# Counting tensor instructions per fetched block in a build-time scheduler, and placing dense matmuls where the next block would be late

## The chip, the cores and the metric

The kernel runs on all eight cores of one Trainium2 chip, one sequence per core; nothing passes between the cores. The metric is the device time in microseconds (us) of the slowest core. Every execution is also recorded core by core: the span from first to last instruction and the granted clock of TensorE.

Executions have two states. In the slow one, the cores of one die (cores 0 to 3 or 4 to 7) show a lower granted clock than the others and the time is longer: the kernel before took 3630.3 us in a fast execution, 3772.86 in one where the four cores of die 0 had a clock of 0.94, and 4275.75 where they had 0.81. Where single cores are compared, they come from *undisturbed dies*, those in which all four cores had a granted clock of 0.981 or more.

Engine names: PE is TensorE's matmul, PEld its weight load, DVE is VectorE, ACT is ScalarE, POOL is GpSimd, SP is SyncE.

## The reference, cut to what matters

Four layers of a hybrid decoder trunk, D = 1024, feed-forward width 2816, 8 prompts of 2048 tokens and 128 single-token samples.

```python
def _layer(x, ...):
    h = _rmsnorm(x, norm1_g)
    z = h @ w_in                          # dense, 1024 -> 4096
    zb, zc, zv, zu, ga, gs = split(z)
    conv_out, new_buf = _conv_causal(zc * zv, conv_buf, conv_w, conv_b)
    ya = zb * conv_out
    ys, hr, hi = _s5(zu, ...)             # diagonal state space: 32 groups, 64 complex states each
    gy = gelu(ys)
    ys = gy * sigmoid(gy @ w_glu + b_glu)
    m = sigmoid(ga) * (ya @ w_branch[:512]) + sigmoid(gs) * (ys @ w_branch[512:])
    x = x + m @ w_out                     # dense
    h2 = _rmsnorm(x, norm2_g)
    gate, up = split(h2 @ w_gate_up)      # dense, 1024 -> 5632
    return x + (silu(gate) * up) @ w_down # dense
    ...
```

Nearly all arithmetic is in the dense products. The state space (SSM) part is little arithmetic in many small matmuls.

## The kernel before

A core works through its 2048 columns in two halves of 1024; the first half also carries 16 sample columns. The kernel's Python code does not emit instructions directly. It records *operations*, each with an estimated duration, its dependences and its buffers. An operation of TensorE is a group of matmuls. `schedule()` then simulates the five engines and fixes every engine's instruction order at build time.

The scheduler picks the ready operation of the best priority that has room for its results:

```python
    def schedule(self):
        ...
        def feasible(o, t):
            ...
                if fr not in tls:     # out of the program's order: keep `reserve` buffers free
                    if p.reserve < 0 or len(free) - len(tls) < p.reserve:
                        return False
            ...
        while nleft:
            ...
                while a and n < 60:
                    item = heapq.heappop(a)
                    o = item[2]
                    n += 1
                    if feasible(o, t):
                        ...
                        pick = o
                        break
                    put.append(item)
            ...
            o = pick
            dur = o.dur
            ...
            o.start = t
            efree[e] = t + dur
            ...

    PP = Pool("psum", 8, lambda s: PSUM[s], reserve=3)
```

There are two kinds of TensorE operation. A dense one has typically 8 matmuls of 128x272, 128x384 or 128x512:

```python
    def proj(parts, blk, own=()):
        ps = PP.new()
        nmm = len(parts)
        subs = []
        for i, (u, kw, c, src, keys) in enumerate(parts):
            subs.append((lambda e, ...: e.matmul(
                ps[:, 0:blk.n], lhsT=u.ap(kw, c), rhs=src(blk), start=(i == 0), stop=(i == nmm - 1)),
                [u.key] + keys(blk) + list(own), MMN(blk.n)))
        S.pe(subs, [(ps,)], FULL)
```

An SSM quarter (four a layer and half) has up to six operations of many tiny matmuls, 152 in all in the first half:

```python
            # L1043: 32 matmuls of 64 columns       L1053: 16 of 16 columns (samples)
            S.pe(subs, [(gg,)], (128, 64))
            ...                                   # DVE: rotate, scan, rotate back
            # L1090/L1093: 16 of 128 and 64 columns L1103/L1107: 24 of 16 columns (samples)
            S.pe(subs, [(yb[0],), (yb[1],)], FULL)
            ...
            # L1117: 64 of 64 columns
            S.pe(subs, [(yb[0],), (yb[1],)], (64, 128))
```

Each matmul is two instructions, a weight load and a multiply (23,772 records of each on core 1 of the kernel before). So 256 instructions are 128 matmuls. By the medians of that core's trace they are 27 us of dense 128x512 ones (216 ns from one to the next), but only 2 to 7 us of the small ones (15 to 56 ns from one to the next).

Of the kernel before, what the change touches and what calls it, by code (L numbers as in the profile page):

```python
# [76 lines left out]
class Prog:  # L77
# [3 lines left out]
    SWITCH = 1.28  # L81
    MODESW = 0.16
    DBW = 300.0e3
    NSEM = {"sp": 14, "pool": 8}

    def __init__(self):
# [91 lines left out]
    def schedule(self):  # L178
        ops = self.ops
        for o in ops:  # L180
            o.succ = []
            o.ready = 0.0
        for o in ops:
            o.npred = len(o.deps)
            for d, i in o.deps:
                d.succ.append((o, i))
        for p in {id(tl.pool): tl.pool for o in ops for tl in o.tiles}.values():
            p.tiles.sort(key=lambda tl: tl.users[0].seq)
        self.order = {e: [] for e in self.ENGS}
        fut = {e: [] for e in self.ENGS}  # L190
        avail = {e: [] for e in self.ENGS}
        efree = {e: 0.0 for e in self.ENGS}
        curset = None
        curmode = None
        lastpe = None
        bus = 0.0
        dcount = {"sp": 0, "pool": 0}
        dlast = {}
        events = []
        ctr = 0  # L200

        def push(t, e):
            nonlocal ctr
            ctr += 1
            heapq.heappush(events, (t, ctr, e))
        for o in ops:
            if o.npred == 0:
                heapq.heappush(fut[o.eng], (0.0, o.seq, o))
        for e in self.ENGS:
            push(0.0, e)  # L210
        nleft = len(ops)
        pos = {e: 0 for e in self.ENGS}
        inorder = {e: [o for o in ops if o.eng == e] for e in self.ENGS}

        def feasible(o, t):
            need = {}
            for tl in o.tiles:
                if tl.slot is None:
                    need.setdefault(tl.pool, []).append(tl)
            for p, tls in need.items():  # L220
                free = p.free
                if len(free) < len(tls):
                    return False
                fr = p.tiles[p.front] if p.front < len(p.tiles) else None
                if fr not in tls:
                    if p.reserve < 0 or len(free) - len(tls) < p.reserve:
                        return False
                elif p.reserve < 0:
                    for k_ in range(len(tls)):
                        if p.tiles[p.front + k_] not in tls:  # L230
                            return False
            return True
        while nleft:
            if not events:
                rem = [o for o in ops if not o.done]
                raise RuntimeError("stuck: %s" % [(o.seq, o.eng, o.npred, [(t.pool.name, t.idx, t.slot) for t in o.tiles]) for o in rem[:12]])
            t, _, e = heapq.heappop(events)
            if isinstance(e, tuple):
                p, s = e
                p.free.append(s)  # L240
                for e2 in self.ENGS:
                    if efree[e2] <= t:
                        push(t, e2)
                continue
            if efree[e] > t + 1e-9:
                continue
            f, a = fut[e], avail[e]
            while f and f[0][0] <= t + 1e-9:
                _, _, o = heapq.heappop(f)
                heapq.heappush(a, (o.prio, o.seq, o))  # L250
            pick = None
            if LISTSCHED:
                put = []
                n = 0
                best_sw = None
                while a and n < 60:
                    item = heapq.heappop(a)
                    o = item[2]
                    n += 1
                    if feasible(o, t):  # L260
                        sw = (e == "act" and o.tset is not None and o.tset != curset)
                        if sw and best_sw is None and n < 6:
                            best_sw = item
                            put.append(item)
                            continue
                        if sw and best_sw is not None:
                            put.append(item)
                            continue
                        if best_sw is not None and o.prio > best_sw[0] + SWW:
                            put.append(item)  # L270
                            break
                        pick = o
                        break
                    put.append(item)
                if pick is None and best_sw is not None:
                    pick = best_sw[2]
                    put.remove(best_sw)
                for item in put:
                    heapq.heappush(a, item)
            else:  # L280
                if pos[e] < len(inorder[e]):
                    o = inorder[e][pos[e]]
                    if a and any(x[2] is o for x in a) and feasible(o, t):
                        a[:] = [x for x in a if x[2] is not o]
                        heapq.heapify(a)
                        pick = o
                        pos[e] += 1
            if pick is None:
                if f:
                    push(f[0][0], e)  # L290
                continue
            o = pick
            dur = o.dur
            if e == "act" and o.tset is not None and o.tset != curset:
                dur += self.SWITCH
                curset = o.tset
            if e == "pe":
                if curmode is not None and o.mode != curmode:
                    dur += self.MODESW
                    o.forced = lastpe  # L300
                curmode = o.mode
                lastpe = o
            o.start = t
            efree[e] = t + dur
            if o.dma:
                q = dcount[e]
                dcount[e] = q + 1
                o.sem = (e, q % self.NSEM[e])
                o.semprev = dlast.get(o.sem)
                dlast[o.sem] = o  # L310
                beg = max(bus, t + dur + 0.6)
                bus = beg + o.nbytes / self.DBW
                o.end = bus + 1.3 + o.extra
            else:
                o.end = t + dur
            o.done = True
            nleft -= 1
            self.order[e].append(o)
            for tl in o.tiles:
                if tl.slot is None:  # L320
                    p = tl.pool
                    tl.slot = p.free.pop(0)
                    tl.prev = p.last[tl.slot]
                    while p.front < len(p.tiles) and p.tiles[p.front].slot is not None:
                        p.front += 1
                tl.left -= 1
                tl.end = max(tl.end, o.end)
                if tl.left == 0:
                    p = tl.pool
                    p.last[tl.slot] = tuple(tl.users)  # L330
                    push(tl.end + self.LAT, (p, tl.slot))
            for s, i in o.succ:
                s.npred -= 1
                r = o.end + (0.0 if e == "pe" and s.eng == "pe" else self.LATPE if s.eng == "pe" else self.LAT) - s.offs[i]
                if r > s.ready:
                    s.ready = r
                if s.npred == 0:
                    heapq.heappush(fut[s.eng], (s.ready, s.seq, s))
                    push(max(s.ready, t, efree[s.eng]), s.eng)
            push(efree[e], e)  # L340
        self.makespan = max(o.end for o in ops)
# [120 lines left out]
def build():  # L462
# [69 lines left out]
    sems = {e: es.enter_context(nc.semaphore(f"s_{e}")) for e in Prog.ENGS}  # L532
    dsems = {(e, i): es.enter_context(nc.semaphore(f"d_{e}{i}")) for e in Prog.NSEM for i in range(Prog.NSEM[e])}

# [892 lines left out]
```

## Time and profile before

| | before |
|---|---|
| time, median of 3 runs | 3630.3 us (3630.3 to 3638.21) |
| span of the slowest core (core 1) and of the fastest | 3626.0 and 3611.5 us |
| PE busy, core 1 | 3473.9 us, 96% |
| PE waits called "issue", core 1 | 22.9 us, 0.6% |
| PE instruction records, core 1 | 51,257 = 200.2 x 256 |

Lines of the profile page of the kernel before, core 1: the span, the busy time of each engine (share of the span, number of instructions), the queue that brings instructions (packets, MB, share of 16 DMA engines), and the chain of waits that ended last.

```profile
span 3626.0 us, 67081 instructions; the slowest of 8 cores (3611.5 to 3626.0 us)
...
PE 3473.9 (96%) x23772; PEld 1960.4 (54%) x23772; DVE 1691.4 (47%) x3029; ACT 1147.2 (32%) x2158; POOL 609.1 (17%) x799
...
q8 instruction: 200, 3.28, 0.4%
...
PE 87%; DVE 4%; issue 4%; DMA 2%; ACT 2%; SPq 1%; DVEq 0%; POOL 0%; ACTq 0%; POOLq 0%
```

The kernel is bound by TensorE, and about 150 us of the span are not PE. The list of PE's waits on core 1 says what ended them; the columns are the total, how often, and the longest.

```profile
PE ps L712 <- ACT H L710: 22.7, 10, 8.9
PE ps L905 <- DVE SC L562: 14.9, 7, 4.3
...
PE ps L670 <- DMA R<-dy: 14.2, 5, 8.9
PE ps L670 <- issue: 7.6, 4, 3.0
...
PE ps L1117 <- issue: 3.5, 1, 3.5
PE ps L1103 <- issue: 3.5, 1, 3.5
PE ps L1053 <- issue: 3.1, 1, 3.1
```

"issue" means that PE waited for nothing that the profile shows. These waits are few and long. The timeline of PE on core 1 shows two of them; the columns are start, duration, line, operation and its tiles, and in brackets the idle time before it.

```profile
586.66 0.19 PE L1107 MATMUL ps<-AS0Z,TAB 128*128 128x16 bf16 x2
590.34 0.18 PE L1103 MATMUL ps<-UU,TAB 128*128 128x16 bf16 x1 [3.48 <-issue]
...
590.74 3.95 PE L670 MATMUL ps<-H,RING 128*128 128x272 bf16 x16
...
595.93 0.82 PE L1117 MATMUL ps<-VT,TAB 64*128 64x64 bf16 x44
600.28 0.47 PE L1117 MATMUL ps<-VT,TAB 64*128 64x64 bf16 x20 [3.53 <-issue]
```

The pauses fall in the *middle* of operations (after 44 of 64 matmuls of one kind), and the profile shows nothing that the next matmul waits for. Counting PE's records from 0, the first instructions after the two pauses are records 9403 (the weight load of the matmul shown) and 9659: exactly 256 apart. All eight pauses of over 1.5 us on core 1 are at records that leave 187 when divided by 256. The queue that brings instructions moved 200 packets of 16,384 bytes each, 3.28 MB in all, for 51,257 records, which is 200.2 blocks of 256. So the trace shows instructions coming in blocks of 256, a packet each. They come while PE works: a packet starts about when the block before its own begins (2.6 us after, see fetchpace). PE paused for over 1.5 us at eight of the 200 block ends on core 1, and each of the eight blocks before these ends is made mostly of small matmuls: 88 to 126 of them, and 2.6 to 7.4 us of work by my estimate, the usual distances of its matmuls in this trace summed (the blocks before the pauses at 600 and 1520 us hold 4.1 and 2.8 us). The block before 600 us in fact took 6.4 us on core 1: after the pause that ends at 590.34, PE's granted clock is 0.60 in 590.7 to 594.8 us, and the 16 matmuls of 128x272 take 3.95 us, against 2.39 us for 16 such at 1512.5 us, where the clock is 1.00.

### The profile page before, as it was taken

To read this page: it belongs to the slowest core of one execution; us is meant where nothing else is said; L and a number is where in the kernel's file an instruction comes from. 1 tells how busy PE (TensorE), PEld (TensorE's weight loads), DVE (VectorE), ACT (ScalarE), POOL (GpSimd) and SP (SyncE) were. 2 spreads that over 40 slices of the span, in tenths; PEclk is the share of its full clock that TensorE was granted. 3 is DMA by queue.
4 is the path that set the end of the run, shared out by engine and by line. 5 is a ranking of instruction groups with operands and counts; after the bars stand their busy time and mean duration, and the time that the engine had idled before them with its cause. 6 is when DMAs were issued, how large, how long until landed. Compare 5 with 4: busy or idle time off the path is not lost.

```text
span 3626.0 us, 67081 instructions; the slowest of 8 cores (3611.5 to 3626.0 us)
## 1 busy us (share of the span) xinstructions
PE 3473.9 (96%) x23772; PEld 1960.4 (54%) x23772; DVE 1691.4 (47%) x3029; ACT 1147.2 (32%) x2158; POOL 609.1 (17%) x799
## 2 busy tenths in 40 slices
PE   6899998999999999999999899999999999999998
PEld 3566666666666666666664344444444444444443
DVE  8856455465554754644245342454214542254423
ACT  4543134432343322533134330233203431142302
POOL 4233210322103221020000200002000110002000
PEclk9899999999999999999999999999999999999999
DMA  8645677445574355854439544574445734464443
GB/s 160 127 71 75 113 156 139 82 71 114 138 148 84 69 115 126 184 123 86 74 60 209 114 82 70 96 171 76 77 75 115 155 67 80 76 138 85 81 70 88
DMA packets 252805, 384.13 MB, mean 106 GB/s; under 512 B 157632, under 2 KB 180800, under 8 KB 246848
## 3 DMA queue, kind: packets, MB, share of 16 engines
q0 software_dynamic: 67968, 243.30, 40.8%
q1 hardware_dynamic: 184512, 136.53, 12.9%
q8 instruction: 200, 3.28, 0.4%
q14 instruction: 125, 1.02, 0.1%
HBM read 567.06 MB, written 56.12 MB: 172 GB/s over the span
## 4 chain that ended last, share of the span: by engine, by line
PE 87%; DVE 4%; issue 4%; DMA 2%; ACT 2%; SPq 1%; DVEq 0%; POOL 0%; ACTq 0%; POOLq 0%
PE ps L670 83%; DMA dy<-YY 1%; PE ps L1117 1%; DVE H L736 1%; ACT SC L1233 1%; PE ps L707 1%; DVE SC L562 1%; PE ps L1043 1%; PE ps L1090 1%; PE ps L918 0%; DMA scv<-CIN 0%; DVE R L1235 0%; SPq L633 0%; PE ps L905 0%; DMA R<-dy 0%
## 5 line engine op out<-in xcount | busy, mean ns | idle before, releaser
L670 PE MATMUL ps<-H,RING 128*128 128x384 bf16 (+2 forms) x12160 | 2196.5, 340 | 30.1 <-DVE H L736 14.2
L670 PEld LDWEIGHTS ps<-H,RING 128*128 128x128 bf16 x12160 | 1191.3, 99 | 973.2 <-issue 57.4
L670 PE MATMUL ps<-R,RING 128*128 128x384 bf16 (+2 forms) x6400 | 1162.4, 338 | 24.2 <-DMA R<-dy 14.2
L670 PEld LDWEIGHTS ps<-R,RING 128*128 128x128 bf16 x6400 | 623.5, 98 | 525.5 <-issue 44.6
L657 POOL DMA_DIRECT2D RING<-wpk x472 | 253.1, 537 | 2588.2 <-PE ps L670 2330.0
L1278 DVE TENSOR_TENSOR R<-SC,ps 128x384 bf16<-128x384 f32 (+2 forms) x440 | 255.1, 583 | 755.0 <-PE ps L670 722.3
L1277 ACT ACTIVATE SC<-ps 128x384 f32<-128x384 f32 (+2 forms) x440 | 225.8, 515 | 1167.9 <-PE ps L670 1152.1
L1256 DVE TENSOR_TENSOR X<-X,ps 128x384 f32<-128x384 f32 (+2 forms) x480 | 271.0, 581 | 386.8 <-PE ps L670 384.8
L705 ACT ACTIVATE SC<-X 128x384 f32<-128x384 f32 (+2 forms) x280 | 147.2, 543 | 205.0 <-DVE X L1256 178.7
L736 DVE SCALAR_TENSOR_TENSOR H<-X,PRM,SC 128x384 bf16<-128x384 f32 (+2 forms) x304 | 190.9, 698 | 27.4 <-ACT SC L717 27.4
L1250 POOL TENSOR_TENSOR R<-TB,SC 128x384 bf16<-128x384 f32 (+1 forms) x160 | 167.8, 1064 | 101.0 <-DVE SC L1247 85.9
L1247 DVE TENSOR_TENSOR SC<-SC,ps 128x384 f32<-128x384 f32 (+1 forms) x160 | 92.7, 584 | 141.4 <-PE ps L670 68.1
L1246 ACT ACTIVATE SC<-ps 128x384 f32<-128x384 f32 (+1 forms) x160 | 81.4, 515 | 235.0 <-PE ps L670 194.9
L1223 DVE TENSOR_TENSOR TB<-TB,ps 128x384 f32<-128x384 f32 (+2 forms) x160 | 90.0, 583 | 128.9 <-PE ps L670 111.3
L562 DVE TENSOR_TENSOR SC<-TB 128x512 f32<-128x512 f32 (+1 forms) x160 | 121.1, 767 | 5.6
L1182 DVE TENSOR_TENSOR CIN<-ps,SC 128x384 f32<-128x384 f32 (+2 forms) x80 | 46.9, 586 | 156.1 <-ACT SC L1181 146.4
L1168 ACT ACTIVATE TB<-ps 128x384 f32<-128x384 f32 (+1 forms) x160 | 79.6, 516 | 100.1 <-PE ps L670 99.7
L562 POOL TENSOR_TENSOR TB<-TB 128x512 f32<-128x512 f32 (+1 forms) x72 | 89.9, 1253 | 69.7 <-DVE TB L562 52.1
L1235 DVE TENSOR_TENSOR R<-R,SC 128x384 bf16<-128x384 bf16 (+2 forms) x80 | 46.8, 588 | 112.9 <-ACT SC L1233 111.3
L562 DVE TENSOR_TENSOR H<-SC 128x384 bf16<-128x384 f32 (+2 forms) x140 | 81.3, 590 | 36.2 <-ACT SC L705 36.2
L909 ACT ACTIVATE TAB<-ps 128x512 bf16<-128x512 f32 x60 | 35.4, 597 | 125.5 <-PE ps L905 125.3
L1181 ACT ACTIVATE SC<-ps 128x384 f32<-128x384 f32 (+2 forms) x80 | 40.9, 512 | 101.3 <-PE ps L670 101.3
(184 smaller groups left out, 1686.2 us busy)
## 6 DMA issues: line engine op xcount, KB each, us to landing
RING<-wpk POOLq DMA_DIRECT2D x440, 512.0 KB, 7.0
TAB<-stash SPq DMA_DIRECT2D x21, 1792.0 KB, 9.3
stash<-TAB SPq DMA_DIRECT2D x15, 1792.0 KB, 8.3
R<-stash SPq DMA_DIRECT2D x7, 1792.0 KB, 13.2
RING<-wpk POOLq DMA_DIRECT2D x32, 384.0 KB, 6.2
du<-R SPq DMA_DIRECT2D x32, 256.0 KB, 8.1
UU<-du SPq DMA_DIRECT2D x32, 256.0 KB, 8.3
dy<-YY SPq DMA_DIRECT2D x32, 256.0 KB, 7.4
```

What stands on the lines that cost most here:

```text
L562: fn = lambda e: e.tensor_tensor(out=out(), in0=a(), in1=b(), op=op)
L657: S.dma("pool", lambda e: e.dma_start(out=t[:, 0:n], in_=wpk[l, ui, :, 0:n]), [("X",) + gate] if gate else (), [(t,)], 128 * n * 4, prio=- ...
L670: subs.append((lambda e, u=u, kw=kw, c=c, src=src, i=i: e.matmul(ps[:, 0:blk.n], lhsT=u.ap(kw, c), rhs=src(blk), start=(i == 0), stop=(i = ...
L705: act(lambda e, kt=kt, t=t: e.activation(out=t[:, 0:n], in_=xin(kt)[0], func=AF.Square), xin(kt)[1], [(t,)], n)
L736: dve(lambda e, kt=kt, xi=xi, g=g: e.scalar_tensor_tensor(out=H[:, kt, blk.c0:blk.c0 + n], in0=xi(), scalar=g, in1=rs[:, 0:n], op0=ALU.mul ...
L1223: dve(lambda e, po=po, n=n, t_=t_, blk=blk: e.tensor_tensor(out=t_[:, blk.c0:blk.c0 + n], in0=t_[:, blk.c0:blk.c0 + n], in1=po[:, 0:n], op ...
L1246: act(lambda e, sg=sg, pg=pg, n=n: e.activation(out=sg[:, 0:n], in_=pg[:, 0:n], func=AF.Sigmoid), [(pg,)], [(sg,)], n, tset="sig")
L1247: dve(lambda e, sg=sg, po=po, n=n: e.tensor_tensor(out=sg[:, 0:n], in0=sg[:, 0:n], in1=po[:, 0:n], op=ALU.mult), [(sg,), (po,)], [(sg,)], n)
L1250: S.op(MENG, lambda e, sg=sg, n=n, t_=t_, blk=blk, j=j: e.tensor_tensor(out=R[:, MT[j], blk.c0:blk.c0 + n], in0=t_[:, blk.c0:blk.c0 + n], ...
L1256: dve(lambda e: e.tensor_tensor(out=X[:, j, blk.c0:blk.c0 + n], in0=X[:, j, blk.c0:blk.c0 + n], in1=ps[:, 0:n], op=ALU.add), [(ps,)] + xke ...
L1277: act(lambda e, sg=sg, pg=pg, n=n: e.activation(out=sg[:, 0:n], in_=pg[:, 0:n], func=AF.Silu), [(pg,)], [(sg,)], n, tset="silu")
L1278: dve(lambda e, sg=sg, pu=pu, n=n, blk=blk, ti=ti: e.tensor_tensor(out=R[:, ti, blk.c0:blk.c0 + n], in0=sg[:, 0:n], in1=pu[:, 0:n], op=ALU ...
```

## The change

Its intent: let the scheduler count instructions, estimate when the next block will have arrived, and when an operation would run into a block not yet there, prefer another operation, so that dense matmuls cover the fetch.

```diff
+    IBLK = 256
+    ILAT = 6.0
...
+        icount = 0
+        ienter = [0.0]
...
+        def istall(o, t):
+            n = 2 * len(o.subs) + 1
+            b = (icount + n) // self.IBLK
+            if b < len(ienter):
+                return 0.0, 0.0
+            x = t + o.dur * (b * self.IBLK - icount) / n
+            land = ienter[b - 1] + self.ILAT if b > 2 else 0.0
+            return max(0.0, land - x), x
...
                 while a and n < 60:
                     item = heapq.heappop(a)
                     o = item[2]
                     n += 1
+                    if stalled is not None and o.prio > stalled[0] + 400:
+                        put.append(item)
+                        break
                     if feasible(o, t):
+                        if e == "pe" and istall(o, t)[0] > 0.05:
+                            if stalled is None:
+                                stalled = item
+                            put.append(item)
+                            continue
...
+                if pick is None and stalled is not None:
+                    pick = stalled[2]
+                    put.remove(stalled)
...
+                st_, x_ = istall(o, t)
+                dur += st_
+                icount += 2 * len(o.subs) + 1
+                if icount // self.IBLK >= len(ienter):
+                    ienter.append(x_ + st_)
```

No matmul, load or other operation is added or removed. The diff puts 31 lines above the kernel proper, so L670 of before is L701 of after, L1107 is L1138, and so on.

More of the change, by code (lines that the diff above doesn't have):

```diff
@@ L255, in schedule @@
                 best_sw = None
+                stalled = None
                 while a and n < 60:
```

## The prediction

> **What bounds the kernel.** TensorE. On the page of the slowest core it is busy 3473.9 of 3626.0 us (96%), and the chain of waits is 87% PE (83% the dense projections). About 150 us are not PE. The list of waits puts the larger part on data: 22.7 us on ACT at the first norm, 14.9 on DVE tables, 14.2 on the norm's DVE, 14.2 on the reload R<-dy. What the change attacks are the waits called "issue" on PE: 24 us on core 1, 16 to 25 on the others, in seven to nine pieces, the longest 3 to 5 us each.
>
> **Are those fetches?** Yes, I think. [...] the instruction queue moved 200 packets, 3.28 MB, and PE has 51,257 records, or 200.2 blocks. In core 1's record, the stalls begin exactly 256 records apart (590.3 and 600.3 us; 1044.7 and 1055.3; 3240.4 and 3250.8), each with a fetch packet inside it or just before. So they aren't hidden there: about 23 us, 0.6%. That is the ceiling. All lie where 64-column matmuls (15 ns pitch) fill a block in 3 to 8 us; a dense 512-column block takes 27 us (216 ns pitch). [...]
>
> **What the change does.** It changes no work: the same 23,772 matmuls, the same loads. It makes the scheduler prefer another tensor operation when the next would enter a late block. Comparing the two built instruction orders, line shifts removed, PE differs only in five stretches, all in the first half, layers 1 to 3: 590-621, 643-661, 1060-1084, 1109-1124, 1515-1525 us. The second half, with its stalls at 2406, 3240 and 3250, keeps its PE order, and so do the blocks before the stalls at 590, 1044 and 1055. So at most the stalls at 600 (3.5 us) and 1520 (2.3 us) can go.
>
> Nor do dense matmuls end up well spread there. Summing measured pitches over real blocks: the block before 600 falls from 4.1 to 3.0 us of work, the next from 4.8 to 4.1; after 1055, 4.9 and 4.8 become 3.7 and 4.1; before 1520, 2.8 becomes 3.9. The scheduler counts from zero, the hardware boundary lies 187 records in; it assumes 6 us, and its small matmuls are shorter than the real ones. The pieces are worth -2 to +3 us each and nearly cancel. The two later stretches swap dense against dense: little, perhaps a microsecond of waiting.
>
> **Prediction.** 3631 us, 8 in 10 between 3618 and 3645. Faster by over 2%: 0.01; within 2%: 0.98; slower by over 2%: 0.01.
>
> **What the profile would show.** PE busy within 10 us of 3474; the issue waits still 16 to 28 us a core, with stalls at 590, 600, 1044, 1055 and in the second half's places; the instruction queue still at 200 packets. From 1670 us to the end, the same span within 5 us. In 576-665 us and 1040-1125 us the stretch is as long as before within 4 us. If I am wrong about fetches, the stalls will move freely and not be multiples of 256 records apart.
>
> **What would make it wrong.** Fetch latency may depend on what the DMA engines do at the moment, so moved small matmuls could meet a fetch of 10 us instead of 6, three times: +10 us. Or the moved dense work hides both stalls and the earlier scans on DVE shorten later waits: -10 us. The reload R<-dy may shift by some us where SyncE's order changed.

The sum: it was the kernel before, 3630.3 us, plus pieces of -2 to +3 us that nearly cancel, which came to 3631. In the warning at the end, 6 us is the constant `ILAT` of the code, and 10 us is about the distance of two successive pauses on core 1 of the kernel before (9.9 to 10.7 us, in three pairs).

## The result and the profile after

| | before | after |
|---|---|---|
| median of the runs side by side | 3632.32 us (3630.3 to 3638.21, 4 runs) | 3640.27 us (3634.08 to 3642.79, 4 runs) |
| ratio of fast runs | | 1.0017, 95% interval 0.9999 to 1.0035 |

A ratio here is the mean time of one kernel's fast runs over that of the other's fast runs of the same rounds, so it is not quite the ratio of the medians quoted.

The same lines of the page of the kernel after, whose slowest core was core 2 (166 matmul records are missing from this trace, hence the lower count):

```profile
span 3637.9 us, 66940 instructions; the slowest of 8 cores (3611.9 to 3637.9 us)
...
PE 3468.2 (95%) x23606; PEld 1964.8 (54%) x23772; DVE 1691.3 (46%) x3029; ACT 1149.6 (32%) x2160; POOL 609.2 (17%) x799
...
q8 instruction: 200, 3.28, 0.4%
...
PE 86%; DVE 4%; issue 3%; DMA 3%; SPq 2%; ACT 1%; DVEq 0%; ACTq 0%; POOL 0%; POOLq 0%
```

PE's waits on that core, in the same columns:

```profile
PE ps L701 <- DMA R<-dy: 23.1, 6, 9.5
PE ps L743 <- ACT H L741: 22.3, 9, 8.9
PE ps L936 <- DVE SC L593: 14.1, 7, 3.7
...
PE ps L701 <- issue: 4.2, 3, 2.9
...
PE ps L1124 <- issue: 3.6, 1, 3.6
```

It is tempting to read a story here: fewer issue waits, more waiting for the reload R<-dy. It would be wrong. These are two different cores, and each was picked *because* it was the slowest of its run. Over the 24 cores of three profiles of each kernel (the first and two repeats, below), R<-dy is 14.0 us before and 14.0 us after, and the issue waits are 20.9 before and 21.2 after. (The equal sums hide two opposite changes: from 100 to 1824 us they fell from 13.2 to 10.6 us, and from 1824 to 2163 us they rose from 0.0 to 2.5.) The page of the slowest core is a sample of one from the unlucky end.

So what did the change do? The timeline of PE on core 1 of the kernel after, at the place shown above:

```profile
589.08 0.18 PE L1134 MATMUL ps<-UU,TAB 128*128 128x16 bf16 x1 [2.11 <-issue]
...
589.76 0.67 PE L1074 MATMUL ps<-UU,R 128*64 128x64 bf16 x31
...
595.77 1.38 PE L1148 MATMUL ps<-VT,TAB 64*128 64x64 bf16 x45 [2.02 <-issue]
597.30 1.97 PE L701 MATMUL ps<-H,RING 128*128 128x272 bf16 x8
```

Both pauses are still there. Instead of the 16 dense matmuls after the first one (590.74 above), the next SSM quarter's 32 *small* matmuls come at once, and dense work comes later. Each pause is shorter here by some 1.4 us, but the first of the two has the same order before it in both kernels, so at least that difference is chance.

The one place where the rule did what its author meant is in layer 3. Timeline of PE, core 1, kernel before:

```profile
1518.33 0.17 PE L1107 MATMUL ps<-AS0Z,R 128*128 128x16 bf16 x1
1520.75 0.18 PE L1107 MATMUL ps<-AS0Z,R 128*128 128x16 bf16 x1 [2.25 <-issue]
```

and kernel after:

```profile
1511.88 0.47 PE L1074 MATMUL ps<-UU,R 128*64 128x64 bf16 x18 [1.71 <-issue]
...
1515.30 2.72 PE L701 MATMUL ps<-H,RING 128*128 128x384 bf16 x8
...
1519.66 0.19 PE L1138 MATMUL ps<-AS0Z,R 128*128 128x16 bf16 x2
```

A dense group of eight stands between the small ones, and the pause in the last of them is gone. (A shorter one has appeared at 1511.88, because the order before it changed too.)

**How often did the rule act?** Recording the scheduler's decisions while it builds, without using any time from it, shows that in the whole program it saw seven late blocks and set an operation aside for another only *three* times. Two of the three that stepped in were themselves small operations, of 16 and 24 matmuls; one was dense. There are three reasons in the code:

- At three of the seven late blocks, no ready dense operation had room when the late one had to be taken: out of the program's order, it must leave three of the eight PSUM banks free (`reserve=3`). At one of the three, all had room until a small operation had stepped in.
- At the other four, close to the block's end, a dense group (17 instructions by the rule's count) itself crosses into the late block, so it is set aside as well.
- Nothing in the rule says that what steps in must be dense.

PE's order differs in five stretches only, all in the first half. In the second half the matmuls come in the same order.

**Where the time went**, by stretch. The stretches are cut at matmuls that stand in the same place in both orders. The numbers are the mean over 24 cores of after minus that over 24 cores of before, with standard errors:

| stretch (us from the start) | after minus before |
|---|---|
| 0 to 589, same order | +0.5 ± 0.5 |
| 589 to 618, rewritten | -0.5 ± 0.3 |
| 639 to 658, rewritten | -0.9 |
| 1054 to 1078, rewritten | +0.4 ± 0.3 |
| 1103 to 1119, rewritten | -1.2 |
| 1510 to 1521, rewritten | -2.6 ± 0.3 |
| 1521 to 1574, same order | +1.6 ± 0.5 |
| 1574 to 1824, same order | 0.0 |
| 1824 to 1979, same order | +1.95 ± 0.65 |
| 1979 to 2163, same order | +1.98 ± 0.6 |
| 2163 to 3607, same order | 0.0 ± 0.9 |
| whole core, mean (3620.5 to 3622.0) | +1.5 |

The rewritten stretches gained 4.8 us by this table (the sum of five rows). The rest gave 5.5 to 6 back. Two places stand out.

*1521 to 1574.* After layer 3's gain, PE soon waits for something it did not wait for so long before. Timeline of PE on core 0, kernel before:

```profile
1553.10 9.82 PE L670 MATMUL ps<-H,RING 128*128 128x384 bf16 x64
1562.75 9.67 PE L670 MATMUL ps<-R,RING 128*128 128x384 bf16 x59
```

and core 1, kernel after:

```profile
1554.65 9.82 PE L701 MATMUL ps<-H,RING 128*128 128x384 bf16 x64
1568.20 6.03 PE L701 MATMUL ps<-R,RING 128*128 128x384 bf16 x21 [3.73 <-ACT SC L1277]
```

The wait is for the sigmoid of the merge's gate on ScalarE (L1246 before, L1277 after), by the code probably for the PSUM bank that it reads. PE's waits for this tile over the whole kernel rise from 1.6 to 3.2 us a core on the mean, about what this stretch lost: more than half of layer 3's 2.6 is given back 50 us later.

*1824 to 2163.* Here the order is the same, yet the mean is 3.9 us longer, and uneven: the spread between cores rises from about 1 us to about 3 in each of the two stretches. The timeline of PE on core 7, kernel before:

```profile
1975.47 0.70 PE L1043 MATMUL ps<-UU,TAB 128*64 128x64 bf16 x32
```

and the same matmuls on core 7, kernel after:

```profile
1972.07 0.24 PE L1124 MATMUL ps<-UU,R 128*128 128x64 bf16 x1 [3.43 <-issue]
...
1981.47 0.63 PE L1074 MATMUL ps<-UU,TAB 128*64 128x64 bf16 x27
1988.31 0.42 PE L1074 MATMUL ps<-UU,TAB 128*64 128x64 bf16 x5 [6.20 <-issue]
```

Two successive blocks come late and cost this core 9.6 us. That happened on 7 of the 24 cores of the kernel after (7 to 10 us each, 2.5 of the 3.9 us by the mean) and on none of 24 before. The experiments below ask why.

### The profile page after: what moved, and what is told of

Same layout as the page of the kernel before. It is cut to its first block, busy times and chain, and to the rows that moved or that the text cites. A ratio compares the mean times of both kernels' runs of the same rounds, so it can differ in the third digit from the quotient of the medians.

```text
span 3637.9 us, 66940 instructions; the slowest of 8 cores (3611.9 to 3637.9 us)
## 1 busy us (share of the span) xinstructions
PE 3468.2 (95%) x23606; PEld 1964.8 (54%) x23772; DVE 1691.3 (46%) x3029; ACT 1149.6 (32%) x2160; POOL 609.2 (17%) x799
## 4 chain that ended last, share of the span: by engine, by line
PE 86%; DVE 4%; issue 3%; DMA 3%; SPq 2%; ACT 1%; DVEq 0%; ACTq 0%; POOL 0%; POOLq 0%
PE ps L701 82%; DMA dy<-YY 2%; PE ps L1148 1%; DVE H L767 1%; PE ps L738 1%; SPq L758 1%; DVE SC L593 1%; PE ps L1074 1%; DMA yT<-X 1%; PE ps L949 1%; ACT SC L1264 0%; DMA R<-dy 0%; PE ps L1121 0%; SPq L1339 0%; PE ps L936 0%
## 5 line engine op out<-in xcount | busy, mean ns | idle before, releaser
L701 PE MATMUL ps<-H,RING 128*128 128x384 bf16 (+2 forms) x12054 | 2186.9, 340 | 37.0 <-DVE H L767 13.5
L701 PEld LDWEIGHTS ps<-H,RING 128*128 128x128 bf16 x12160 | 1191.0, 98 | 972.2 <-issue 57.8
L701 PE MATMUL ps<-R,RING 128*128 128x384 bf16 (+2 forms) x6342 | 1164.1, 339 | 38.8 <-DMA R<-dy 23.1
L701 PEld LDWEIGHTS ps<-R,RING 128*128 128x128 bf16 x6400 | 626.3, 98 | 539.3 <-issue 59.3
L1278 DVE TENSOR_TENSOR SC<-SC,ps 128x384 f32<-128x384 f32 (+1 forms) x160 | 92.8, 584 | 150.6 <-ACT SC L1277 74.4
L1277 ACT ACTIVATE SC<-ps 128x384 f32<-128x384 f32 (+1 forms) x160 | 81.4, 515 | 243.3 <-PE ps L701 211.7
```

The costliest lines, as they stand in the source:

```text
L701: subs.append((lambda e, u=u, kw=kw, c=c, src=src, i=i: e.matmul(ps[:, 0:blk.n], lhsT=u.ap(kw, c), rhs=src(blk), start=(i == 0), stop=(i = ...
L1277: act(lambda e, sg=sg, pg=pg, n=n: e.activation(out=sg[:, 0:n], in_=pg[:, 0:n], func=AF.Sigmoid), [(pg,)], [(sg,)], n, tset="sig")
L1278: dve(lambda e, sg=sg, po=po, n=n: e.tensor_tensor(out=sg[:, 0:n], in0=sg[:, 0:n], in1=po[:, 0:n], op=ALU.mult), [(sg,), (po,)], [(sg,)], n)
```

## The experiments

Three theories were put to the test.

- **Theory A (fetch, and small action).** The issue waits are late instruction blocks. The rule removes one or two of them, worth 2 to 5 us, and the chain of waits behind gives most of it back.
- **Rival B.** The pauses are not fetches but belong to the operations (a change of array mode, or a semaphore that the profile does not show), so where a block ends does not matter.
- **Rival C.** Fetches matter, and the rule is only badly tuned: with its faults mended, the 21 us could be had.

Twelve runs were made, on three chips: the two kernels again (twice each), and seven variants, one of them twice. All gave correct results.

| kernel | mean span on undisturbed dies (us) | before, same chip | ratio of fast runs (95%) |
|---|---|---|---|
| before_again | 3621.8 ± 0.7 | 3622.7 ± 0.5 | 0.9985 (0.9952 to 1.0018) |
| after_again | 3622.8 ± 1.2 | 3622.7 ± 0.5 | 1.0014 (0.9977 to 1.0052) |
| shift128 | 3618.4 ± 1.1 | 3622.7 ± 0.5 | 0.9968 (0.9925 to 1.0010) |
| only_l3 | 3623.2 ± 1.7 | 3623.5 ± 0.6 | 1.0021 (0.9952 to 1.0090) |
| only_l12 | 3620.3 ± 1.3 | 3623.5 ± 0.6 | 1.0042 (0.9997 to 1.0087) |
| repaired | 3625.8 ± 1.3 | 3623.5 ± 0.6 | 1.0028 (0.9947 to 1.0110) |
| fill_all | 3626.0 ± 1.5 | 3623.5 ± 0.6 | 0.9989 (0.9927 to 1.0050) |
| before_third | 3622.0 ± 0.7 | 3622.2 ± 0.6 | 0.9992 (0.9961 to 1.0024) |
| after_third | 3623.8 ± 1.3 | 3622.2 ± 0.6 | 0.9998 (0.9966 to 1.0031) |
| relabel | 3622.2 ± 0.8 | 3622.2 ± 0.6 | 1.0000 (0.9964 to 1.0036) |
| shift128_again | 3617.4 ± 0.9 | 3622.2 ± 0.6 | 0.9983 (0.9934 to 1.0031) |

The mean span averages the cores of all undisturbed dies of a kernel's runs; it shows differences of a tenth of a per cent that the metric, a maximum over eight cores, does not. Its standard error (±) is taken from the means of single dies. fetchpace does other work and is left out.

### The two kernels again: before_again, after_again

No edit.

> The kernel before, unchanged, against itself: how far one program strays from itself. If the 7.7 us that the second half and the transition cost in the changed kernel's profile are chance (transfers of eight cores colliding differently in each execution), this run's profile should also show stretches from 1824 us on that differ between cores and from the first profile by some us, and a ratio of 1.000 with an interval of 0.002 or so. If the loss is a property of the changed program, the eight cores here again agree within 1 to 2 us in each stretch, and the sum of the second half is within 2 us of the first profile.

> The changed kernel again, with its second profile. Chance: ratio to before 1.000 to 1.001, and the cores that were slow between 1824 and 2163 us in the first profile (0, 2, 6, 7) are not the same ones now. Property of the program: ratio 1.0015 to 1.0030 and the second half again 6 to 10 us longer than before. In both, the rewritten stretches (590-618, 639-658, 1054-1078, 1103-1119, 1510-1521 us) together 3 to 5 us shorter than before, as in the first profile.

The medians are 3630.41 us for before_again and 3638.53 for after_again. The ratios of both hold 1 in their intervals, and the mean cores agree within 1 us. But the slowest core of undisturbed runs averages 3634.3 us after, against 3631.2 for the kernel before and 3629.0 for before_again. The cores spread more after: the four cores of a die differ by a standard deviation of 7.7 and 8.2 us in the two repeats, against 5.6 to 6.7 for the kernel before, and the means of single dies by 3.9 and 4.6, against 1.8 to 2.6. The maximum of eight rises with the spread. So the few us that the medians show are mostly spread and hardly the mean. In two of the three profiles the slowest core is one with the late blocks at 1960 to 2000 us; in the first (core 2) it is not. So the uneven stretch explains this in part only. Nor is such a rise this kernel's alone: the slowest core of relabel, below, averages 3634.8 us too, with no such blocks in its profile.

### Shifting where the blocks end: shift128

The kernel before, with 128 waits that are already satisfied put behind PE's first operation. The work and its order stay; every block boundary moves by half a block.

```diff
-            for o in self.order[e]:
+            for n_, o in enumerate(self.order[e]):
+                if e == "pe" and n_ == 1:
+                    for _ in range(128):
+                        eng.wait_ge(sems["act"], 1)
```

> The kernel before with 128 waits on an already reached semaphore put at the head of the tensor stream, where TensorE waits for the first norm anyway: every later instruction moves by half a block. If the stalls are fetches of 256-instruction blocks, they leave their instructions: the first instruction after each stall is again number 187 modulo 256 of the new stream, so 59 modulo 256 of the old one; from summed pitches the short blocks are then 37, 66, 67, 96, 97, 163 (3.2, 3.7, 3.3, 2.8, 4.5, 4.8 us of work), and the stalls at old records 9403, 9659, 17083, 37307 and 47291 vanish. Issue waits still 16 to 28 us a core and the time within 0.3% of before. If the stalls belong to the instructions (a semaphore that the profile misses, a mode change of the array), they stay where they were, at L1103, L1117, L1053, L1093.

The pauses moved. The seven old places other than 600 us (590.3, 1044.7, 1055.3, 1520.8, 2406.5, 3240.4 and 3250.8 us) are clean. Three of the pauses that core 1 has now, from the timeline of PE (lines are 3 higher than in the kernel before):

```profile
600.32 3.89 PE L673 MATMUL ps<-H,RING 128*128 128x384 bf16 x14 [3.29 <-issue]
...
1510.22 0.19 PE L1096 MATMUL ps<-UU,TAB 128*128 128x64 bf16 x1 [3.32 <-issue]
...
2824.91 0.29 PE L1093 MATMUL ps<-UU,R 128*128 128x128 bf16 x1 [4.69 <-issue]
```

Counting the 128 waits as instructions, each pause again begins at an instruction that leaves 187 when divided by 256. This decides against B: the same operations at the same places no longer pause, and others do, in the block's rhythm. One of them stops inside a dense group of 128x384 matmuls, after two of 16, where the form of the array is 128*128 before and after.

The traces also hold the fetches themselves: every packet of the instruction queue q8, with its start and length. On core 1 of the kernel before, one packet lands at 589.06 us and PE goes on at 590.34; the next lands at 598.70 and PE goes on at 600.28. Over the 24 cores of the kernel before, each of the 159 pauses of over 1.5 us ends 1.06 to 1.64 us after such a packet has landed (148 pauses after: 1.20 to 1.65), although these packets are 18 us apart on the mean. So the pauses are fetches.

The added waits take time at the start (13.5 us of "issue" on core 1), mostly in place of a wait for data: what PE waits for ACT's H fell from 23.1 to 12.6 us, and the stretch 0 to 589 us lost only 2.3. In spite of that the mean core is 4.3 us *faster* than before, the clearest such difference of any variant. It was therefore run again, as shift128_again.

### The pace of fetching by itself: fetchpace

The kernel before, with ten blocks' worth of 16-column matmuls (1280) put in twice: at the very start, while inputs and weights are loaded, and in the second half in layer 2, when little is being transferred. Its own result is thrown away.

```diff
+    def burst(n, prio, src):
+        ps = PP.new()
+        S.pe([(lambda e, i=i: e.matmul(ps[:, 0:16], lhsT=ONESB[:], rhs=ONESB[:, 0:16], start=(i == 0), stop=(i == n - 1)),
+               [C_("ONESB")] + src, MMN(16)) for i in range(n)], [(ps,)], FULL, prio)
...
+    burst(1280, -3000, [])
...
+            if half == 1 and l == 2:
+                burst(1280, None, hkeys(7, BLKS[1][1]))
```

> The kernel before with two bursts of 1280 matmuls of 16 columns each, ten blocks of nothing but small work (25 ns pitch, so 3.2 us a block if nothing else binds), one at the start while the first inputs load, one in the second half among the weight loads of layer 2. Fetch theory: each block of a burst takes the fetch's own time, 5 to 10 us, the burst 50 to 100 us in place of 32, with a pause at every 256th instruction and nowhere else; the busier DMA of the second burst gives the longer pauses. If blocks are not fetched one at a time in step with execution (a deep buffer), the first several blocks of a burst run at 3.2 us and pauses come only later, or never.

The timeline of PE on core 1 in the first burst:

```profile
1.48 5.93 PE L1328 MATMUL ps<-ONESB 128*128 128x16 bf16 x217 [1.48 <-DVE HC L592]
11.92 3.56 PE L1328 MATMUL ps<-ONESB 128*128 128x16 bf16 x128 [4.51 <-issue]
19.76 3.56 PE L1328 MATMUL ps<-ONESB 128*128 128x16 bf16 x128 [4.28 <-issue]
27.05 3.56 PE L1328 MATMUL ps<-ONESB 128*128 128x16 bf16 x128 [3.73 <-issue]
30.78 3.56 PE L1328 MATMUL ps<-ONESB 128*128 128x16 bf16 x128 [0.17 <-issue]
37.80 3.56 PE L1328 MATMUL ps<-ONESB 128*128 128x16 bf16 x128 [3.46 <-issue]
```

and in the second:

```profile
2828.48 3.58 PE L1328 MATMUL ps<-ONESB 128*128 128x16 bf16 x128 [0.16 <-issue]
2832.23 7.05 PE L1328 MATMUL ps<-ONESB 128*128 128x16 bf16 x256 [0.16 <-issue]
2839.72 3.58 PE L1328 MATMUL ps<-ONESB 128*128 128x16 bf16 x128 [0.44 <-issue]
```

The windows of the two bursts on core 1; the columns are the stretch, its length, busy time of PE, PEld, DVE, ACT and POOL, PE's clock, the DMA engines' busy share, and GB/s:

```profile
10.00:46.00 36.00, 18.98 (x685) 18.63 (x685) 27.66 (x54) 13.05 (x31) 15.41 (x15) 1.00 0.92 192
2818.00:2853.00 35.00, 33.84 (x1248) 33.30 (x1245) 0.00 (x0) 0.33 (x2) 0.00 (x0) 0.58 0.02 4
```

Each row of 128 matmuls is one block. With the DMA engines 92% busy, blocks follow one another every 7.0 to 7.8 us (19.76 minus 11.92, 37.80 minus 30.78), about half of it pause, though one came in time. One more block of this burst is late (44.82), and the two after it come in time (48.55 and 52.27). With the DMA engines 2% busy, they follow every 3.7 us with no more than 0.2 us between them, except 0.44 once. So a block took at most 3.7 us to come in the second burst, and mostly about twice that in the first. The scheduler's constant of 6.0 us is right for neither. (My expectation had the loads of the two bursts the wrong way round: I took the second for the busier. The trace decides; the argument needs only that they differ. Its 5 to 10 us for a fetch are an estimate: blocks that ended in a pause took 4.8 to 11.2 us on six cores of the kernel before. Its 25 ns are the median distance of the 16-column matmuls of L1107 there.)

The first burst also says how far fetching runs ahead. 217 matmuls, 434 instructions, went without a pause, after the first instructions of the program; then five of the next six blocks came late. 434 instructions and those first ones, about two blocks of 256, are what ran here before a block came late. The packets agree: over the 18 cores of the kernel before whose records are complete, a block's packet starts 2.6 us after the first instruction of the block *before* it (median; nine in ten between -2.2 and 8.5 us), so about one block ahead. Where a pause ends, the packet itself took only 0.9 to 2.6 us: what varies most is when it starts.

The kernel's own time (3702.76 us in its one fast run) is that of the added matmuls and has no other use here.

### One part of the change alone: only_l3, only_l12

The rule is switched on only after, or only until, 1300 us of the scheduler's own clock.

```diff
-                        if e == "pe" and istall(o, t)[0] > 0.05:
+                        if e == "pe" and (t > 1300.0) and istall(o, t)[0] > 0.05:     # only_l3; only_l12: t <= 1300.0
...
-                dur += st_
+                dur += st_ if (t > 1300.0) else 0.0
```

> The rule of the changed kernel switched on for layer 3 of the first half only; the tensor order then differs from before in one stretch, 1516-1525 us. If the parts act where they stand, 1510-1521 us is 2 us shorter than before, 1521-1574 us 1.5 to 2.5 us longer (the gate projection then waits for the SSM output on its way through DRAM, which comes no sooner), the other first-half stretches are within 0.5 us of before. If the second half's loss (1824-2163 us, 4.8 us on the mean of eight cores, in two profiles) hangs on this last rewritten stretch, it is here too, 3 to 6 us; if it hangs on the earlier ones or on the sum of the moves, 1824-2163 us is within 1 us of before and no core stalls on a fetch at 1970-1995 us.

> The rule switched on for layers 1 and 2 only; the tensor order differs in four stretches, 591-621, 643-661, 1060-1083 and 1109-1124 us, and is that of before from there on. Parts act where they stand: 639-658 us 0.9 us shorter, 1103-1119 us 1.2 us shorter, 590-618 and 1054-1078 us within 1 us; 1510-1574 us as before. The second half's loss: here if it hangs on layers 1 and 2, absent (within 1 us) if on layer 3.

only_l3 repeats layer 3's exchange: the stretch 1510 to 1521 us is 2.28 us shorter than before, and 1521 to 1574 is 1.89 longer. So giving back most of the gain 50 us later follows from the local move alone, not from what happened in layers 1 and 2. only_l12 repeats the two dense-for-dense swaps (639 to 658: -0.94; 1103 to 1119: -1.17) and leaves layer 3 as it was (+0.06).

As whole kernels neither is resolved: 3623.2 ± 1.7 and 3620.3 ± 1.3 us for the mean core, beside 3623.5 ± 0.6. (only_l12's difference is 2.3 standard errors, from four dies alone: in each of its four runs one die was disturbed.) only_l12's metric, at 1.0042, points the other way from its mean core, and two of its cores, on a disturbed die, lost much in a stretch whose order did not change. I count it as inconclusive.

### The rule with its faults mended: repaired

The kernel after, with three changes: the count starts at 69, so that the scheduler's blocks end where the trace shows the real ones to end (256 minus 187); while something is set aside, another operation may go down to one free PSUM bank; and only an operation of at most 8 matmuls may step in.

```diff
-        icount = 0
+        icount = 69
-        def feasible(o, t):
+        def feasible(o, t, res=None):
-                    if p.reserve < 0 or len(free) - len(tls) < p.reserve:
+                    if p.reserve < 0 or len(free) - len(tls) < (p.reserve if res is None else min(res, p.reserve)):
-                    if feasible(o, t):
-                        if e == "pe" and istall(o, t)[0] > 0.05:
+                    if feasible(o, t, None if stalled is None else 1):
+                        if e == "pe" and (istall(o, t)[0] > 0.05 or stalled is not None and len(o.subs) > 8):
```

> The changed kernel with three faults of its rule mended: the count starts at 69, where the chip's first block begins; only a dense operation (at most 8 matmuls) may step in for a late one; and it may take the PSUM banks down to one free, not three. The tensor order differs from before in 596-609, 1060-1085, 1513-1528 and 1532-1534 us only. The short blocks grow: 36 from 4.1 to 5.3 us of work, 66 and 67 from 4.9 and 4.8 to 5.4 and 5.1, 97 from 2.8 to 5.8 (96 shrinks from 4.8 to 2.8). If spreading removes stalls, the stretches 590-618, 1054-1078 and 1510-1521 us lose 1 to 3 us each against before and boundary stalls in the first half fall by 3 to 6 us a core; the time is still within 0.3% of before, since some of it is given back at the next wait for the SSM output. If the latency of a fetch, not the spread, sets the stalls, the sums do not move by more than 1.5 us.

The issue waits did not fall: 23.1 us a core, against 20.9 before and 21.2 after. (From 100 to 1824 us they did, from 13.2 to 11.6 us, less than the fall of 3 to 6 us that the expectation named; after 1824 us they rose by 3.8.) The mean core is 2.3 us slower than before (3625.8 ± 1.3 against 3623.5 ± 0.6), which is not resolved. In layer 3 the stretches 1510 to 1521 and 1521 to 1574 together are 0.5 us shorter; the cut between them lies inside a part that this kernel rewrites, so its two halves can't be judged apart. Five of its eight cores had pauses of 3.3 to 4.7 us in the second half at 1960 to 2000 us. A rule that waits for the moment when a block is *predicted* to be late needs a fetch time good to a microsecond or two (my estimate, from pauses of 1.5 to 3.5 us on core 1 before), and in fetchpace a block took at most 3.7 us with the DMA engines 2% busy and mostly 7.0 to 7.8 with them 92% busy. That explains how such a rule can miss; that it is what made this one miss, no run shows. It goes against half of rival C: mending these three faults was not enough.

### Dense work after every large group of small matmuls: fill_all

The other half of C: do the pauses cost what they last? This variant of the kernel before has no model of fetching. After every TensorE operation of 16 matmuls or more, the next pick is the best ready operation of 4 to 8 matmuls that has room under the usual reserve, within 400 of the best priority.

```diff
+            if e == "pe" and owed > 0:
+                best = None
+                for item in a:
+                    o = item[2]
+                    if len(o.subs) <= 8 and len(o.subs) >= 4 and o.prio < top_prio(a) + 400 and feasible(o, t, 3):
+                        if best is None or item < best:
+                            best = item
+                if best is not None:
+                    pick = best[2]
...
+                owed = 1 if len(o.subs) >= 16 else max(0, owed - 1)
```

> The idea taken literally, without any count: after each tensor operation of 16 or more small matmuls the scheduler takes one dense operation if one is ready, everywhere, in all layers and both halves. Summed pitches over real blocks say that the work missing to 6.5 us a block falls from 27 to 21 us in total, and to 8 us from 65 to 56 us. If dense matmuls in between hide fetches for free, boundary stalls fall from 24 to 10-16 us a core and the time by 6 to 12 us. If they only shift the waiting, because the SSM chain then starts and ends later, the stalls fall as much but waits on the SSM output (R<-dy, ACT SC, CIN) grow by as much or more, and the time is the same or up to 0.5% longer.

It did to the waits what the change was meant to do. The issue waits fall from 20.9 to 7.2 us a core, by two thirds. The time did not follow: 0.9989 (0.9927 to 1.0050) for the metric, and 3626.0 ± 1.5 us for the mean core against 3623.5 ± 0.6 before. Two of its four runs were slow, so the metric alone would be weak evidence; the mean core over undisturbed dies is the better one, and it is not faster.

Where did 13.7 us go? PE's list of waits answers in part, by the mean over its eight cores against the 24 of before. All waits together fell by only 4.8 us (113.6 to 108.8). DVE's SC became shorter too (14.9 to 9.2 us). New or longer are waits for other tiles: ACT's CONVST 0 to 3.2 us, DVE's R 3.2 to 6.4, ACT's R 1.1 to 4.1, DVE's CTM 0 to 2.6, ACT's TB 0.5 to 2.4, together 13.9 us. And the stretch 0 to 589 us, where the kernel before has only 1.2 us of issue waits a core, became 7.7 us longer. The SSM quarter is a chain (small matmuls, rotation and scan on VectorE, small matmuls, gelu, and so on). A dense group put between its links delays what VectorE and ScalarE begin next; that is how I read these waits, from the code. Lines of the list of core 0 of fill_all (lines are 16 higher than in the kernel before):

```profile
PE ps L1133 <- issue: 4.3, 3, 1.6
PE ps L921 <- ACT CONVST L1206: 3.6, 1, 3.6
...
PE ps L921 <- ACT R L802: 2.9, 1, 2.9
```

The longest of these pauses of issue is 1.6 us, and the list of core 1 before has neither of the two waits for ScalarE. So the removed pauses came back as other waits for the larger part. But the waits still fell by 4.8 us and the mean core did not get shorter. The traces show where the rest is. PE uses its array in three forms here (128*128, 128*64 and 64*128 in the timelines), and a change of form left it idle for 0.14 us on the mean (23.5 us at 174 changes in the kernel before), below the 0.15 us from which the list counts a wait. fill_all changes form 222 times, the kernel before 174 times; the short idle times at these changes sum to 30.3 us against 23.5 (cores with complete records). These 6.8 us more outweigh the 4.8 us of waits saved.

### Is it the buffers? relabel, with both kernels again

In the second half the kernel after has before's PE order, but the buffers that operations use are numbered differently, and in PE's stream one wait fewer stands (51,256 instructions by the order, against 51,257), so that blocks end one instruction earlier. To see whether buffer numbers alone bring the late blocks at 1960 to 2000 us, relabel is the kernel before with its buffer views permuted.

```diff
-    PP = Pool("psum", 8, lambda s: PSUM[s], reserve=3)
-    RP = Pool("ring", NRING, lambda s: RING[:, s, :], reserve=-1)
+    PP = Pool("psum", 8, lambda s: PSUM[(3 * s + 1) % 8], reserve=3)
+    RP = Pool("ring", NRING, lambda s: RING[:, (s + 2) % NRING, :], reserve=-1)
...                                               # seven more pools alike
```

> The kernel before with its schedule untouched and only its buffers renamed (PSUM banks, weight ring, scratch and table slots permuted), as the changed kernel's buffers come to be in the second half, where its order is that of before. If where the buffers lie makes the second half slower, 1824-2163 us is 3 to 6 us longer than in before's profile of this call. If not, it is the same within 1.5 us, as is the mean span of cores on undisturbed dies.

> The kernel before once more, for a third profile of eight cores and for spans of its cores on the chip of the next three runs. If the second half's loss in the rewritten kernels is theirs, 1824-1979 us is again 155.4 us within 0.5, and no core stalls on a fetch at 1970-1995 us. If it is an event that can hit any version, some cores here show it (158 us and more). Mean span of the cores on undisturbed dies 3621 to 3624 us.

> The changed kernel a third time. Mean span of the cores on undisturbed dies 3622 to 3625 us, within 2 us of before in the same call, as on the other chip (3622.8 against 3622.7 and 3621.8); the median of the slowest core 3 to 8 us above before, because cores differ more. In the profile the rewritten stretches are together 4 to 5 us shorter than before and 1521-1574 us about 2 us longer.

relabel behaves as before does: 3622.2 ± 0.8 us for the mean core, +0.2 and +0.5 us in the two stretches from 1824 to 2163, and late blocks at 1960 to 2000 us on none of 8 cores. after_third has them on two of 8 (10.0 and 8.3 us); before_third on none. So the late blocks do belong to the kernel after. That buffer numbers do not bring them is likely and not shown: at 7 in 24, eight cores show none by chance in 6 of 100 cases, and relabel's numbers are not those of the kernel after. The metric of after_third is 0.9998 (0.9966 to 1.0031), the same as before.

What does bring them stays open. The order of PE is the same there, and the boundary differs by one instruction. only_l3 had them on one core of 8 (8.8 us), only_l12 on two (3.2 us, and 4.6 us at 2010 us on a core that ran late; both on the disturbed die), repaired on five. The packets of q8 show which step is late. On core 7 of the kernel after, the packets of the two late blocks start 8.3 and 13.6 us after the first instruction of the block before, and then take 0.9 and 1.1 us; on core 7 of the kernel before, the same two start after 3.0 and 4.6 us. In the 13.6 us the DMA engines were 93% busy, but they were 94% busy in the 4.6 us too, so the load alone does not decide. What held these packets back, no run here shows.

### The half-block shift again: shift128_again

The file of shift128, on another chip.

> The half-block shift again: cores on undisturbed dies were 3618.4 us on the mean, 4 us less than before on the same chip. If where the block boundaries fall is worth that much, the mean is again 3 to 5 us below before here; if it was a draw, within 1.5 us. The stalls again at the shifted places (block 38, 67, 68, 97, 165).

The mean core is 3617.4 ± 0.9 us, against 3622.2 ± 0.6 for before: 4.8 us faster, and 4.3 on the first chip. So the gain of 0.12 to 0.13% for the mean core is reproduced. In the metric it is not resolved: 0.9983 (0.9934 to 1.0031), and 0.9968 (0.9925 to 1.0010) the first time. In undisturbed runs the slowest core averages 3627.8 us against 3630.4 for before here, and 3625.8 against 3631.2 there.

Where it comes from is clear only in part. After the first 100 us the issue waits are 14.2 us a core, against 20.9 before: the shift put several block ends where dense work covers them, for example three between 2163 and 3607 us (2.81, 1.51 and 3.04 us on core 1 before) for one of 4.69, and that stretch gained 4.6 us (16 cores against 24 of before). 658 to 1054 gained 6.6 us and 1510 to 1521 gained 3.9; 1054 to 1078 lost 4.05, 1119 to 1510 lost 3.5, 0 to 589 lost 2.3, and 1824 to 2163 lost 2.2. All of PE's waits together, with those at the start, are 114.2 us against 113.6, which looks like no gain. But up to 100 us they are 4.3 us longer while PE's busy time there is 4.1 us shorter, and after 100 us they are 3.6 us shorter (74.4 against 78.0), which is the gain of these profiles (3617.0 against 3620.5 us a core). Note the contrast with fill_all: there 13.7 us of pauses went by moving work, and nothing was gained; here 6.7 us went without moving any, and the mean core gained 4 to 5. That fits the theory that it is the reordering that gives the gain back (by longer waits for other engines, and by the changes of array form counted above), but two variants do not prove it.

So this is a version that beats both kernels by its mean core. In the metric no such gain is resolved, and it is a draw of block ends and not a rule: any later edit draws again.

## Why the prediction was right

The prediction was 3631 us (3618 to 3645), within 2%, and the result was 3640.27 us with a ratio of 1.0017: inside the range, and the same class. Point by point:

- **"What bounds the kernel: TensorE."** Right, and unchanged: PE 96% before, 95% after, with 166 records missing from the latter.
- **"Are those fetches? Yes, I think."** Right, shown by shift128 (all pauses moved, in step with the block) and by fetchpace.
- **"Fetch latency may depend on what the DMA engines do at the moment."** A good warning: in fetchpace a block took at most 3.7 us with the DMA engines 2% busy, and mostly 7.0 to 7.8 with them 92% busy; core 7 of the kernel after took 16.2 from one late block to the next (1988.31 minus 1972.07). No single figure would do: over the six cores with complete records in the first profile of the kernel before, a block that ended in a pause of over 1.5 us took 4.8 to 11.2 us where the one before it had ended without one (30 cases), and 7.8 to 11.0 us where it had not (9 cases).
- **"It changes no work... five stretches, all in the first half."** Right, read from the built orders.
- **"At most the stalls at 600 and 1520 can go."** The one at 1520 went (1510 to 1521: -2.6 us). The one near 600 did not: core 1 paused 2.02 us at 595.77.
- **"Its small matmuls are shorter than the real ones."** Wrong. Set beside the trace, the scheduler's small matmuls agree: a block that it takes for 3.19 us has 3.2 us of summed pitches. What keeps the rule from acting is the room kept in PSUM, the crossing of the dense group itself, and that small operations may step in.
- **"The pieces are worth -2 to +3 us each and nearly cancel."** Mis-sized. The rewritten stretches together are -4.8 us. What cancels them lies elsewhere: +1.6 us in layer 3's output projection, where PE waits for ScalarE, and +3.9 us in the second half.
- **"From 1670 us to the end, the same span within 5 us."** Right for the mean (+3.9 us up to 2163, 0.0 ± 0.9 after), but not for single cores: in 7 of 24, two late blocks alone cost 7 to 10 us.
- **"The issue waits still 16 to 28 us a core."** Right as a mean (21.2 us; single cores range from 15.8 to 32.6), and the instruction queue still has 200 packets.
- **"That is the ceiling", 23 us.** This is the step that would have failed in another case. The sum of the pauses is not what removing them is worth: fill_all removed 13.7 us of them and the kernel did not get faster: 8.9 us came back as other waits, and 6.8 us were added by changes of array form.

So the outcome was called for the right main reason, that the rule hardly acts. The belief that its small effects cancel *locally* was wrong: they are a small local gain, given back later. That the two came out nearly equal, so that the whole stayed within 1.5 us by the mean core, was foreseen by no step of the prediction: so far it was luck.

## What to carry to other kernels

Before costing a scheduling rule, build both orders and count what it moved: here a rule with a plausible aim set three operations aside in a program of 23,772 matmuls, and only one of them for dense work. A pause that you can see and name is not yet a gain: ask which chain sets the next wait, and remove the pause in a crude variant (as fill_all does) before refining the rule that removes it. Differences of a tenth of a per cent are judged by the mean over many cores and by stretches cut at the same instructions, not by the slowest core's page, which is picked for being unlucky.
